# Separate tiles for the output halves, and the SSD high and low parts in one tile per group, in a hybrid LRU, attention and SSD layer

## Chip, cores and metric

The kernel runs on one core of a Trainium2 chip. The metric is the device time of one launch in microseconds: 2015.51 is the median of three runs (2010.99 to 2017.05).

## What is computed

One layer of a hybrid model for 2048 prompt tokens and 32 sample tokens (8 sequences of 4). After an RMS norm the input goes through one projection; an RG-LRU branch, a dilated attention branch and an SSD branch work on its parts, and a last projection joins them. The part that matters here, cut from the reference:

```
y, h = ssd_chunked(xs, dt, A, bm, cm, h0)          # chunks of 128 tokens, 16 heads of 64, 2 groups
ys = y + ssd_d[:, None] * xs
yg = (ys * silu(z)).reshape(B, L, 2, 512)
yg = yg * rsqrt(mean(yg * yg, axis=-1) + EPS)      # per group
y_ssd = yg.reshape(B, L, 1024) * ssd_norm_g
mix = concatenate([y_lru, y_attn, y_ssd], -1) @ w_out      # 2048 x 1024
out = x + rmsnorm(mix, post_g)
```

The outputs are `out` for prompt and samples, and new states, among them the last SSD state `ssd_h_p`.

## The kernel before

The first stages project the tokens, run the LRU and the convolutions, and the attention, and leave their results in DRAM (`d_y` for LRU and attention, `d_xbc`, `d_z`, `d_cum` for the SSD). The last stage, from about 1450 us on, does two things at once for 16 chunks of 128 tokens.

`ssd_part(c)` (from L1234) computes the SSD of chunk c in 15 steps: one to open (`ssd_open`: L669 `gp`, L672 `gm`, L678 `tpb`), then seven for each of two groups of 8 heads. In a group: `ssd_decay` loads `sg` (L649), makes `ecB` from it on ScalarE (L695) and the decay matrix (L697, L699, L700); `ssd_x` transposes and scales x (L710 to L715); TensorE makes `yd` and `yo` (L1251, L1256); VectorE forms `y` in four steps from `yo`, `ecB`, `yd`, `xb` and the gate `zt` (L1264 to L1267); `group_norm` squares it on ScalarE (L721), adds on POOL (L722, L723) and sums over partitions with a matmul by ones, `rs` (L726); then `stp` renews the state `hT` (L1273 to L1279), and the second half of `group_norm` scales `y` (L730). Last, ScalarE casts `y` to its high part (L1288) and VectorE subtracts for the low part (L1289).

`out_chunk(c)` (from L1385) multiplies the mixed features of chunk c by `w_out`, in high and low parts, three matmuls a step (`mm3`, L82 to L84). There are 32 steps, 16 blocks of 128 features for each of two halves of 512 output columns; steps 0 to 15 take LRU and attention (k below 8, both halves), steps 16 to 31 the SSD (k from 8 on, both halves). Each half is squared on ScalarE (L1445). Then comes the norm (L1448, L113, L114), and for each half an output tile `ot` is filled (L1459), the residual `xres` is added (L1460) and the tile is stored (L1461). The last chunk has its own form (L1408, L1455). `last_state` (L1463) transposes `hT` and stores it through `ho` (L1468 to L1470), for each of two groups, in step 24 of the last chunk.

The order: 15 steps of `ssd_part` go with the 32 of `out_chunk`, so the second group of chunk c is finished in the first steps of `out_chunk(c)` and the first group of chunk c + 1 in its last steps. This is the order in which the program is written. The framework plans each engine's queue when it builds the program: it takes instructions by their place in the program, but passes over those whose inputs or buffers are not ready yet in its plan. The order of each queue is fixed after that, and on the chip each engine waits at an instruction until its inputs are there.

Buffers: pool `ck` gives each tag two buffers unless told otherwise. Tag `yt` is shared by `y` of `ssd_part` and by the output tiles `ot`. `sh` and `sl` hold the high and low parts of both groups of a chunk, 4 KB per partition each. `x` holds the residuals (and raw weights at the stage's start), two buffers. `ho` has one buffer of its own.

```
y = ck.tile([128, 4, 128], F32, tag="yt", name="y")
ot = ck.tile([128, 512], F32, tag="yt", name="ot")
mh = ck.tile([128, 8, 128], F32R, tag="sh", name="sh")
h_, l_ = (mh, ml) if k < 8 else chunks[c]
ho = ck.tile([128, 4, 128], F32, tag="ho", name="ho", bufs=1)
```

Of the kernel before, what the change touches and what calls it, by code (L numbers as in the profile page):

```python
# [8 lines left out]
F32 = mybir.dt.float32  # L9
F32R = mybir.dt.float32r  # L10
AF = mybir.ActivationFunctionType
OP = mybir.AluOpType
# [20 lines left out]
def tile_hybrid_step(ctx: ExitStack, tc: tile.TileContext, A):  # L33
    nc = tc.nc
    act, dve, pool, pe, sp = nc.scalar, nc.vector, nc.gpsimd, nc.tensor, nc.sync
# [45 lines left out]
    def mm3(out, wh, wl, xh, xl, start, stop):  # L81
        pe.matmul(out, lhsT=wh, rhs=xh, start=start, stop=False)  # L82
        pe.matmul(out, lhsT=wh, rhs=xl, start=False, stop=False)  # L83
        pe.matmul(out, lhsT=wl, rhs=xh, start=False, stop=stop)  # L84
# [578 lines left out]
    def ssd_open(c, ck, ps, msk):  # L663

        t0, n = TT[c]
        bc = load_bc(ck, c)
        gp = ps["y"][0].tile([128, 2, 128], F32, tag=ps["y"][1], name="gp")
        for g in range(2):
            pe.matmul(gp[:n, g, :n], lhsT=bc[:, g], rhs=bc[:, 2 + g], start=(g == 0), stop=(g == 1),  # L669
                      skip_group_check=True)  # L670
        gm = ck.tile([128, 2, n], F32, tag="gm", name="gm", bufs=1)
        dve.tensor_tensor(out=gm[:n], in0=gp[:n, :, :n], in1=msk[:n, None, :n].to_broadcast([n, 2, n]), op=OP.mult)  # L672
        if c == 16:
            return bc, gm
        tp = ps["t"][0].tile([128, 4, 128], F32, tag=ps["t"][1], name="tpb")
        bt = ck.tile([128, 2, 128], F32, tag="bt", name="bt", bufs=1)
        for g in range(2):
            pe.transpose(tp[:, g], bc[:, g], ident)  # L678
        act.copy(out=bt, in_=tp[:, 0:2])
        return bc, gm, bt  # L680
# [51 lines left out]
    def load_z(ck, c, g):  # L732
        return load_rows4(ck, c, g, "zt", d_z)
# [6 lines left out]
    with tc.tile_pool(name="cks", bufs=1) as ck:  # L740
        ps = {"t": (psT, "tp"), "y": (psG, "g")}
# [224 lines left out]
    wo = {}  # L966
# [241 lines left out]
    chunks = {}  # L1208
# [25 lines left out]
    def ssd_part(c):  # L1234
        ck = ck0 if c == 0 else late["ck"]
        ps6 = {"t": (psA, "mm"), "y": (psA, "mm")} if c == 0 else late["ps6"]
        bc, gm, bt = ssd_open(c, ck, ps6, late["tri0" if c == 0 else "tri"])
        yield
        for g in range(2):
            hs = slice(8 * g, 8 * g + 8)  # L1240
            ecB = None if c == 0 else ck.tile([128, 4, 128], F32, tag="ecB", name="ecB", bufs=1)
            sg = ssd_decay(c, g, ck, gm, ecB)
            yield
            xb, xdt, xte = ssd_x(c, g, ck, ps6)
            pool.tensor_tensor(out=xb, in0=xb, in1=dF[:, 4 * g:4 * g + 4, None].to_broadcast([128, 4, 128]), op=OP.mult)
            yield
            hT = late["hT"]
            yd = psA.tile([128, 4, 128], F32, tag="mm", name="yd")
            for m in range(4):
                for e in range(2):  # L1250
                    pe.matmul(yd[64 * e:64 * e + 64, m], lhsT=xdt[:, 2 * m + e], rhs=sg[:, 2 * m + e],  # L1251
                              start=(m == 0), stop=(m == 3), skip_group_check=True)

            yo = None if c == 0 else psA.tile([128, 4, 128], F32, tag="mm", name="yo")
            for m in range(4 if c else 0):
                pe.matmul(yo[:, m], lhsT=hT[:, g, 128 * m:128 * m + 128], rhs=bc[:, 2 + g],  # L1256
                          start=(m == 0), stop=(m == 3), skip_group_check=True)
            yield
            zt = load_z(ck, c, g)
            y = ck.tile([128, 4, 128], F32, tag="yt", name="y")  # L1260
            if c == 0:
                dve.tensor_tensor(out=y, in0=yd, in1=xb, op=OP.add)
            else:
                dve.tensor_tensor(out=y, in0=yo, in1=ecB, op=OP.mult)  # L1264
                dve.tensor_tensor(out=y, in0=y, in1=yd, op=OP.add)
                dve.tensor_tensor(out=y, in0=y, in1=xb, op=OP.add)
            dve.tensor_tensor(out=y, in0=y, in1=zt, op=OP.mult)  # L1267
            yield
            norm = group_norm(ck, ps6, y, 128, dve if c == 0 else pool)
            next(norm)  # L1270
            yield
            stp = psA.tile([128, 512], F32, tag="mm", name="stp")
            pe.matmul(stp, lhsT=bt[:, g], rhs=xte.rearrange("p h d -> p (h d)"), start=True, stop=True)  # L1273
            if c == 0:
                act.copy(out=hT[:, g], in_=stp)
            else:
                hv = hT[:, g].rearrange("p (h d) -> p h d", d=64)
                pool.tensor_tensor(out=hv, in0=hv, in1=dec[:, c, hs, None].to_broadcast([128, 8, 64]), op=OP.mult)
                dve.tensor_tensor(out=hT[:, g], in0=hT[:, g], in1=stp, op=OP.add)  # L1279
            yield  # L1280
            for _ in norm:
                pass
            if g == 0:
                mh = ck.tile([128, 8, 128], F32R, tag="sh", name="sh")
                ml = ck.tile([128, 8, 128], F32R, tag="sl", name="sl")
                chunks[c] = mh, ml
            kk = slice(4 * g, 4 * g + 4)
            act.copy(out=mh[:, kk], in_=y)  # L1288
            dve.tensor_tensor(out=ml[:, kk], in0=y, in1=mh[:, kk].bitcast(F32), op=OP.subtract)  # L1289
            yield  # L1290

    ssd = (None for c in range(16) for _ in ssd_part(c))
# [29 lines left out]
    for i in range(16):  # L1322
# [3 lines left out]
        n = [0, 0]  # L1326
# [29 lines left out]
    ck = es.enter_context(tc.tile_pool(name="ck", bufs=2))  # L1356
# [28 lines left out]
    def out_chunk(c):  # L1385
        smp = c == 16
        t0, n = TT[c]
        if not smp:
            mh = c1.tile([128, 8, 128], F32R, tag="mh", name="mh")
            ml = c1.tile([128, 8, 128], F32R, tag="ml", name="ml")  # L1390
            for k0 in (0, 4):
                ym = load_rows4(ck, c, k0 // 4, "ym", d_y, 1)
                kk = slice(k0, k0 + 4)
                act.copy(out=mh[:, kk], in_=ym)
                dve.tensor_tensor(out=ml[:, kk], in0=ym, in1=mh[:, kk].bitcast(F32), op=OP.subtract)
        ops, ots, xres = [], [], []
# [7 lines left out]
        def scaled(hf):  # L1404

            sl = slice(512 * hf, 512 * hf + 512)
            ots.append(ck.tile([128, 512], F32, tag="yt", name="ot"))
            dve.tensor_tensor(out=ots[hf], in0=ops[hf], in1=pgB[:, sl], op=OP.mult)  # L1408
            residual(hf)

# [3 lines left out]
        for hf in range(2 if smp else 0):  # L1414

            sl = slice(512 * hf, 512 * hf + 512)
            pq = psA.tile([128, 512], F32, tag="mm", name="pq")
            for k in range(4):
                for i in range(2):
                    for j in range(4):  # L1420
                        kk = 4 * j + k
# [5 lines left out]
            ps = psO.tile([128, 512], F32, tag="o", name="ops")  # L1427
# [5 lines left out]
        for hf, k in () if smp else order:  # L1433
            if cnt[hf] == 0:
                ops.append(psO.tile([128, 512], F32, tag="o", name="ops"))
            ps = ops[hf]
            sl = slice(512 * hf, 512 * hf + 512)
            h_, l_ = (mh, ml) if k < 8 else chunks[c]
            mm3(ps[:n], h_[:, k % 8, :n], l_[:, k % 8, :n], wo[k][0][:, sl], wo[k][1][:, sl],
                cnt[hf] == 0, cnt[hf] == 15)  # L1440
            cnt[hf] += 1
            yield
            if cnt[hf] == 16:
                jk = ck.tile([128, 512], F32, tag="zt", name="jk")
                act.activation(out=jk[:n], in_=ps[:n], func=AF.Square, accum_out=oss[:n, hf:hf + 1])  # L1445
                if c == 15:
                    scaled(hf)
        dve.tensor_tensor(out=oss[:n, 0:1], in0=oss[:n, 0:1], in1=oss[:n, 1:2], op=OP.add)  # L1448
        r = rstd_of(sm, oss[:, 0:1], DM, n, "ro")
        for hf in range(2):  # L1450
            sl = slice(512 * hf, 512 * hf + 512)
            dst = A["y_prompt"][0, t0:t0 + n, sl] if not smp else A["y_sample"].rearrange("b l d -> (b l) d")[:, sl]
            if c == 15:
                ot = ots[hf]
                dve.scalar_tensor_tensor(out=ot, in0=ot, scalar=r, in1=xres[hf], op0=OP.mult, op1=OP.add)  # L1455
            else:
                residual(hf)
                ot = ck.tile([128, 512], F32, tag="yt", name="ot")
                dve.scalar_tensor_tensor(out=ot[:n], in0=ops[hf][:n], scalar=r[:n], in1=pgB[:n, sl], op0=OP.mult, op1=OP.mult)  # L1459
                dve.tensor_tensor(out=ot[:n], in0=ot[:n], in1=xres[hf][:n], op=OP.add)  # L1460
            sp.dma_start(out=dst, in_=ot[:n])  # L1461

    def last_state():  # L1463
        for g in range(2):
            tp = psT.tile([128, 4, 128], F32, tag="tp", name="tpf")
            for j in range(4):
                pe.transpose(tp[:, j], hT[:, g, 128 * j:128 * j + 128], ident)
            ho = ck.tile([128, 4, 128], F32, tag="ho", name="ho", bufs=1)  # L1468
            act.copy(out=ho, in_=tp)
            sp.dma_start(out=A["ssd_h_p"][0, 0, 8 * g:8 * g + 8].rearrange("(m e) p n -> (e p) m n", e=2), in_=ho)  # L1470

# [9 lines left out]
    for c in range(16):  # L1481
        k = 0
# [115 lines left out]
```

## Time and profile before

| what | value |
|---|---|
| median of three runs | 2015.51 us (2010.99 to 2017.05) |
| the profiled execution | 2012.49 us, span 2010.6 us |
| busy TensorE, VectorE, ScalarE, POOL | 1925.6, 1066.6, 742.7, 279.2 us |
| mean DMA rate over the span | 110 GB/s |
| mean granted TensorE clock | 0.990 |

The span is the time from the first to the last instruction of the program; all times in the rows count from its start. The profile names an instruction by its line in the kernel, its engine, and the tiles it writes and reads. PE is TensorE, DVE VectorE, ACT ScalarE, SP the engine that issues the DMAs here.

### The profile page before, as it was taken

How to read it: one execution, taken by the hardware profiler on the slowest of the kernel's cores; microseconds unless marked ns; L12 is line 12 of the kernel's file. 1: busy time of each engine (PE TensorE's matmuls, PEld its weight loads, DVE VectorE, ACT ScalarE, POOL GpSimd, SP SyncE). 2: the span in 40 equal slices, each digit the busy share in tenths (PEclk: the TensorE clock that was granted, in tenths of full speed). 3: DMA queues.
4: the chain of work that ended last, by engine and by line, in shares of the span. 5: the costliest groups of instructions: out<-in, count | busy, mean ns of one | idle time of the engine just before them, and what ended most of it. 6: DMA issues, size and time to landing. Idle time of an engine off the chain costs nothing.

```text
span 2010.6 us, 35818 instructions
## 1 busy us (share of the span) xinstructions
PE 1925.6 (96%) x14218; PEld 1569.0 (78%) x14218; DVE 1066.6 (53%) x2314; ACT 742.7 (37%) x1464; POOL 279.2 (14%) x346
## 2 busy tenths in 40 slices
PE   7999999999999999999999889999988999989998
PEld 7998888888888888887877667777756777567776
DVE  7315433434323666664223236666767676566664
ACT  6311525252422222223234235556543333333332
POOL 0100101111001111110001000000122232222221
PEclk9999999999999999999999999999999999999999
DMA  8322111111233222225377664334554434234341
GB/s 244 116 75 62 54 54 59 48 61 55 87 93 97 66 73 71 78 69 158 106 208 206 185 176 129 101 102 133 166 157 132 129 112 129 83 108 130 110 126 63
DMA packets 277106, 221.75 MB, mean 110 GB/s; under 512 B 33458, under 2 KB 233122, under 8 KB 276940
## 3 DMA queue, kind: packets, MB, share of 16 engines
q1 hardware_dynamic: 276940, 219.47, 36.2%
q8 instruction: 112, 1.84, 0.4%
q14 instruction: 54, 0.44, 0.1%
HBM read 150.55 MB, written 68.86 MB: 109 GB/s over the span
## 4 chain that ended last, share of the span: by engine, by line
PE 70%; DVE 9%; DMA 8%; ACT 6%; issue 4%; POOL 2%; SPq 1%; DVEq 0%; POOLq 0%; ACTq 0%
PE mm L82 15%; PE mm L83 15%; PE mm L84 15%; PE pt L1142 3%; DMA out_dram<-ot 2%; PE o L1178 2%; ACT sr L1114 2%; PE s L1087 2%; PE ops L83 2%; PE ops L84 2%; PE ops L82 2%; PE s L1066 1%; PE mmt L82 1%; PE mmt L83 1%; PE mmt L84 1%
## 5 line engine op out<-in xcount | busy, mean ns | idle before, releaser
L82 PE MATMUL mm<-xh,wh 128*128 128x512 f32 (+2 forms) x1600 | 563.9, 352 | 0.0
L83 PE MATMUL mm<-xl,wh 128*128 128x512 f32 (+2 forms) x1600 | 560.9, 351 | 0.0
L84 PE MATMUL mm<-xh,wl 128*128 128x512 f32 (+2 forms) x1600 | 560.2, 350 | 0.0
L82 PEld LDWEIGHTS mm<-xh,wh 128*128 128x128 f32 x1600 | 301.6, 188 | 40.7 <-issue 2.9
L83 PEld LDWEIGHTS mm<-xl,wh 128*128 128x128 f32 x1600 | 301.4, 188 | 39.8 <-issue 2.5
L84 PEld LDWEIGHTS mm<-xh,wl 128*128 128x128 f32 x1600 | 300.7, 188 | 38.7 <-issue 1.2
L146 POOL TENSOR_TENSOR wr<-wr,gC 128x1024 f32<-128x1024 f32 x40 | 78.7, 1967 | 398.1 <-DMA wr<-in_w_in_dram 351.4
L439 DVE SCALAR_TENSOR_TENSOR o<-u,ssdc,o 128x512 f32<-128x512 f32 (+1 forms) x216 | 122.8, 590 | 5.1
L148 DVE SCALAR_TENSOR_TENSOR wl<-wr,wh 128x1024 fp32r<-128x1024 f32 x40 | 48.9, 1223 | 120.4 <-ACT wh L147 120.4
L1114 ACT ACTIVATE sr<-sr,nm 128x384 f32<-128x384 f32 (+3 forms) x128 | 97.9, 771 | 23.3 <-DVE nm L1110 14.1
L619 ACT ACTIVATE o<-o 128x512 f32<-128x512 f32 (+2 forms) x60 | 33.1, 552 | 149.9 <-DVE o L439 78.0
L437 DVE TENSOR_SCALAR o<-u,ssdc 128x512 f32<-128x512 f32 (+1 forms) x72 | 47.2, 669 | 65.0 <-ACT u L419 56.8
L1025 ACT COPY ptsb<-pt 128x512 f32<-128x512 f32 x96 | 52.4, 583 | 75.4 <-PE pt L1142 75.3
L82 PE MATMUL mmt<-wh,xh 128*128 128x256 f32 (+3 forms) x272 | 79.2, 293 | 1.0 <-ACT xh L250 0.6
L695 ACT ACTIVATE ecB<-sg 64x512 f32<-64x512 f32 x60 | 37.8, 630 | 113.3 <-DVE y L1264 92.7
L84 PE MATMUL mmt<-wh,xl 128*128 128x256 f32 (+3 forms) x272 | 78.4, 289 | 0.0
L83 PE MATMUL mmt<-wl,xh 128*128 128x256 f32 (+3 forms) x272 | 77.9, 288 | 0.0
L1142 PE MATMUL pt<-ident,sr 128*128 128x128 f32 x576 | 75.2, 281 | 2.3 <-ACT sr L1114 1.8
L1142 PEld LDWEIGHTS pt<-ident,sr 128*128 128x128 f32 x576 | 63.7, 143 | 14.6 <-issue 8.8
L697 DVE TENSOR_SCALAR sg<-sg,cum 128x128 f32<-128x128 f32 (+1 forms) x256 | 70.0, 337 | 5.4 <-ACT ecB L695 5.2
L1087 PE MATMUL s<-k,q 64*32 64x256 f32 (+1 forms) x1536 | 68.9, 348 | 3.8 <-DVE mx L1075 3.2
L1091 DVE CUSTOM_DVE_ANT_0 sr<-s,bias 128x128 f32<-128x128 f32 (+3 forms) x128 | 58.8, 486 | 25.2 <-PE s L1087 24.1
(534 smaller groups left out, 3565.4 us busy)
## 6 DMA issues: line engine op xcount, KB each, us to landing
wr<-in_w_in_dram SPq DMA_DIRECT2D x40, 512.0 KB
sg<-d_cum SPq DMA_DIRECT2D x30, 512.0 KB
d_xbc<-o SPq DMA_DIRECT2D x36, 256.0 KB
x<-in_x_prompt_dram SPq DMA_DIRECT2D x32, 256.0 KB
vt<-in_cache_attn_v_dram SPq DMA_DIRECT2D x32, 256.0 KB
kc<-in_cache_attn_k_dram SPq DMA_DIRECT2D x32, 256.0 KB
xres<-in_x_prompt_dram SPq DMA_DIRECT2D x32, 256.0 KB
out_dram<-ot SPq DMA_DIRECT2D x32, 256.0 KB
```

Source lines behind the costliest of these rows:

```text
L82: pe.matmul(out, lhsT=wh, rhs=xh, start=start, stop=False)
L83: pe.matmul(out, lhsT=wh, rhs=xl, start=False, stop=False)
L84: pe.matmul(out, lhsT=wl, rhs=xh, start=False, stop=stop)
L146: pool.tensor_tensor(out=wr, in0=wr, in1=gC[:, :, None].to_broadcast([128, 8, 128]), op=OP.mult)
L148: dve.scalar_tensor_tensor(out=wl, in0=wr, scalar=scale, in1=wh.bitcast(F32), op0=OP.mult, op1=OP.subtract)
L439: dve.scalar_tensor_tensor(out=o, in0=v(t), scalar=w[:, t:t + 1], in1=o, op0=OP.mult, op1=OP.add)
L697: dve.tensor_scalar(out=sg[:n, h], in0=sg[:n, h], scalar1=cum[:n, c, 8 * g + h:8 * g + h + 1], scalar2=0.0, op0=OP.subtract, op1=OP.min)
L1025: act.copy(out=out, in_=in_)
L1087: pe.matmul(ps[e][32 * n:32 * n + 32, 256 * h:256 * h + m], lhsT=qr[hd[e], r, 32 * n:32 * n + 32], rhs=krs[h][hd[e], r, 0:m // 32], start= ...
L1091: dve.tensor_tensor_reduce(out=sr[e][r][:, :nk], in0=ps[e][:, :nk], in1=bs[:, e, 512 - nk:512], scale=1.0, scalar=NEG, op0=OP.add, op1=OP. ...
L1114: act.activation(out=sr[e][r], in_=sr[e][r], func=AF.Exp, bias=nm[:, e, r:r + 1], accum_out=ll[:, e, r:r + 1])
L1142: pe.transpose(tp[:, r], sr[e][r][:, 128 * g:128 * g + 128], ident)
```

## The change

It touches the last stage alone. The output tiles `ot` get a tag of their own, with two buffers, in both places where they are made. The high and low parts get one tile per group instead of one per chunk: two buffers for the first group, one for the second; the matmuls pick the tile of the group. `ho` takes the tag `x`, with its two buffers, in place of its own. Per partition the parts shrink from 16 to 12 KB, the output tiles add 4 KB, and `ho` gives up 2 KB.

```diff
-            if g == 0:
-                mh = ck.tile([128, 8, 128], F32R, tag="sh", name="sh")
-                ml = ck.tile([128, 8, 128], F32R, tag="sl", name="sl")
-                chunks[c] = mh, ml
-            kk = slice(4 * g, 4 * g + 4)
-            act.copy(out=mh[:, kk], in_=y)
-            dve.tensor_tensor(out=ml[:, kk], in0=y, in1=mh[:, kk].bitcast(F32), op=OP.subtract)
+
+            mh, ml = [ck.tile([128, 4, 128], F32R, tag=f"s{i}{g}", name=f"s{i}", bufs=2 - g) for i in "hl"]
+            chunks[c, g] = mh, ml
+            act.copy(out=mh, in_=y)
+            dve.tensor_tensor(out=ml, in0=y, in1=mh.bitcast(F32), op=OP.subtract)
...
-            ots.append(ck.tile([128, 512], F32, tag="yt", name="ot"))
+            ots.append(ck.tile([128, 512], F32, tag="ot", name="ot"))
...
-            h_, l_ = (mh, ml) if k < 8 else chunks[c]
-            mm3(ps[:n], h_[:, k % 8, :n], l_[:, k % 8, :n], wo[k][0][:, sl], wo[k][1][:, sl],
+            h_, l_ = (mh, ml) if k < 8 else chunks[c, k // 4 - 2]
+            j = k if k < 8 else k % 4
+            mm3(ps[:n], h_[:, j, :n], l_[:, j, :n], wo[k][0][:, sl], wo[k][1][:, sl],
...
-                ot = ck.tile([128, 512], F32, tag="yt", name="ot")
+                ot = ck.tile([128, 512], F32, tag="ot", name="ot")
...
-            ho = ck.tile([128, 4, 128], F32, tag="ho", name="ho", bufs=1)
+            ho = ck.tile([128, 4, 128], F32, tag="x", name="ho", bufs=2)
```

## Rows read from the trace of the kernel before

**Rows 1.** The page, part 1: busy time, share of span, instructions per engine.

```profile
PE 1925.6 (96%) x14218; PEld 1569.0 (78%) x14218; DVE 1066.6 (53%) x2314; ACT 742.7 (37%) x1464; POOL 279.2 (14%) x346
```

**Rows 2.** Windows: stretch, length, busy time by engine, granted clock, DMA share, GB/s.

```profile
1505.00:1981.00 476.00, 443.79 (x2428) 337.26 (x2427) 324.14 (x600) 165.25 (x337) 134.72 (x143) 0.99 0.38 116
1632.00:1664.00 32.00, 30.60 (x167) 23.77 (x167) 22.82 (x43) 11.44 (x23) 9.64 (x11) 1.00 0.39 120
1781.00:1817.00 36.00, 32.00 (x167) 24.83 (x166) 22.79 (x43) 11.53 (x23) 9.49 (x11) 0.95 0.36 111
```

**Rows 3.** Waits from 1500 to 2000 us: total, times, longest.

```profile
DVE y L1264 <- DMA out_dram<-ot: 37.0, 12, 5.2
PE rs L726 <- POOL sq L723: 30.6, 28, 3.6
DVE y L1264 <- PE yo L1256: 13.5, 13, 1.1
DVE y L1264 <- PE ops L84: 7.6, 3, 2.6
```

**Rows 4.** Timeline of one chunk: start, length, instruction, idle before.

```profile
1599.63 1.54 DVE L1460 TENSOR_TENSOR ot<-ot,xres 128x512 f32<-128x512 f32 x2
...
1600.60 0.95 SPq L1461 DMA_DIRECT2D out_dram<-ot  x2
...
1603.85 0.69 DVE L1264 TENSOR_TENSOR y<-yo,ecB 128x512 f32<-128x512 f32 x1 [2.67 <-DMA out_dram<-ot]
...
1608.90 0.51 POOL L723 TENSOR_TENSOR sq<-sq 128x128 f32<-128x128 f32 x1
...
1609.47 0.49 PE L726 MATMUL rs<-sq,ones 128*128 128x128 f32 x2 [0.99 <-POOL sq L723]
```

**Rows 5.** Timeline of TensorE: some `rs` with idle time before them.

```profile
1517.35 0.49 PE L726 MATMUL rs<-sq,ones 128*128 128x128 f32 x2 [2.36 <-POOL sq L723]
...
1530.74 0.49 PE L726 MATMUL rs<-sq,ones 128*128 128x128 f32 x2 [1.01 <-POOL sq L723]
...
1793.14 0.49 PE L726 MATMUL rs<-sq,ones 128*128 128x128 f32 x2 [3.56 <-POOL sq L723]
...
1972.12 0.49 PE L726 MATMUL rs<-sq,ones 128*128 128x128 f32 x2 [0.37 <-POOL sq L723]
...
1988.80 0.38 PE L726 MATMUL rs<-sq,ones 128*128 128x128 f32 x1 [0.32 <-POOL sq L723]
```

**Rows 6.** The chain that ended last, from 1500 us: start, length, what.

```profile
1584.24 3.84 DMA sg<-d_cum
...
1600.60 3.12 DMA out_dram<-ot
...
1781.71 5.70 DMA out_dram<-ot
...
1981.09 2.05 DMA out_dram<-ot
```

**Rows 7.** Windows of 6 us after two idle stretches, columns as in rows 2.

```profile
1793.00:1799.00 6.00, 5.86 (x24) 4.84 (x25) 3.27 (x5) 2.67 (x5) 1.06 (x2) 0.72 0.00 0
...
1576.00:1582.00 6.00, 4.60 (x25) 3.96 (x26) 4.49 (x8) 2.84 (x6) 2.56 (x4) 1.00 0.11 33
```

**Rows 8.** Timeline of the last chunk: residual loads, second `ho`, last adds.

```profile
1982.09 0.95 SPq L1402 DMA_DIRECT2D xres<-in_x_prompt_dram  x2
...
2001.66 0.59 ACT L1469 COPY ho<-tpf 128x512 f32<-128x512 f32 x1 [2.44 <-DMA out_dram<-ho]
...
2005.98 1.42 DVE L1455 SCALAR_TENSOR_TENSOR ot<-ot,rstd,xres 128x512 f32<-128x512 f32 x2 [0.60 <-ACT rstd L114]
```

**Rows 9.** Timeline of a chunk with a store of 4.57 us: SP, VectorE, ScalarE.

```profile
1662.14 1.57 SPq L649 DMA_DIRECT2D sg<-d_cum  x1
...
1664.08 1.28 DVE L1460 TENSOR_TENSOR ot<-ot,xres 128x512 f32<-128x512 f32 x2
...
1670.21 1.28 ACT L695 ACTIVATE ecB<-sg 64x512 f32<-64x512 f32 x2 [7.49 <-DVE y L1264]
```

## The prediction

> **What bounds the kernel now.** I read the page first: TensorE is busy 96% of the span, VectorE 53% [rows 1]. The last quarter is the output stage, where the change lies, so I took it by windows: from 1505 to 1981 us TensorE stands for 32.2 of 476 us. A plain chunk lasts 32 us with 30.6 busy; some last 36, at a mean granted clock of 0.95 [rows 2]. Then the waits of that stretch [rows 3]: VectorE's first multiply of `y` (L1264) waits 37.0 us in 12 times for the landing of an output store, and TensorE waits 30.6 us in 28 times for the squares that feed `rs` (L726). Three more waits of L1264, 7.6 us, stand under a matmul, but they follow a store in the same way, so I count 15.
>
> How the two belong together shows in one chunk [rows 4]. VectorE ends the last output add at 1601.17; `y` shares its two buffers with the output tiles, so it waits for a store issued at 1600.60 and starts at 1603.85, 2.67 us idle. From there, four VectorE steps, the square on ScalarE and two POOL adds lead to `rs` at 1609.47, where TensorE has stood 0.99 us. TensorE is the bound, and this chain is the one that reaches it late.
>
> The idle time follows the store one for one [rows 4 to 6]: a store of 5.70 us gives 3.56, of 3.12 gives 0.99, of 2.05 gives 0.32. In the plain chunks it is the store less 2.13 us: `rs` stands at a fixed place in TensorE's queue, behind the matmul of wo4h, chosen when the program was built, and a store of 2.13 us would just keep up with it.
>
> **The change part by part. The output tiles get buffers of their own (L1407, L1458).** `y` then waits only for the `y` two groups before and starts when VectorE is free, at 1601.17 instead of 1603.85. What goes: the 15 idle stretches ahead of the second group's `rs`, from 2.36 us (the first) to 0.32 (the last) [rows 5]. They sum to 22.9 us: the other 13 of the 28 sum to 7.7, from 1.01 to 0.37, and 30.6 - 7.7 = 22.9. That is 1.53 each.
>
> Not all of it goes. The planner that orders the queues will see `y` ready earlier too and will put `rs` further forward, so what is left is by how much its chain without a store lags behind the plan. No row shows that. The lower bound is 0. The upper one is about 1.0, the largest idle of an `rs` that no store gates. The nearest rows are those first-group `rs` of the plain chunks, whose wait includes a load of `ym` instead: 0.37 to 0.57 in nine of the 13. I take 0.45. The gain is 15 x (1.53 - 0.45) = **16.2 us**, between 8 and 23.
>
> **The clock.** Behind the idle stretches of 2.36, 2.44, 3.56 and 2.60 us the granted clock over 6 us is 0.72, which is a stretch at the lower level, 1.2 GHz; behind one of 2.79 us it stays at 1.00 [rows 7]. One costs 0.28 x 6 = 1.7 us, four 6.7. All four stand behind long stores. Taken as gone: **6.7 us**, between 3.4 (two stay) and 6.7.
>
> The size of the store can be weighed against a page. The rows have stores of 2.05 to 5.70 us between issue and the release of `y`. The Trainium skill, DMA: Bandwidth & Descriptors, section Anatomy of one DMA — SWDGE (gpsimd) path, gives a fixed 2.0 us plus the bytes over 436 GB/s, so 2.6 us is its estimate for 256 KB, if it holds for stores that SP issues. By that each idle stretch would be 2.6 - 2.13 = 0.5 us, 7 us in all with no long store and no clock to win back, and the forecast would be no better than 2006. The rows decide against it.
>
> **High and low parts in two tiles per group (L1284 to L1289, L1438).** The casts, subtractions and matmuls stay the same in number and shape. The second group has one buffer, so its cast (L1288) must follow the last matmul of the chunk before that reads it. That matmul is the last of its chunk and lies before the output adds of 1599.63; `rs`, which the cast needs through `y`, runs on the same TensorE queue at 1609.47 [rows 4]. The order holds already, by almost 10 us. Cost 0; at most a semaphore more per group on VectorE, whose idle time covers it. The first group keeps two buffers.
>
> **The last state (L1468) on the buffers of the residual.** Now the second `ho` is copied at 2001.66, after the first has been stored, and both residual loads of the last chunk were issued at 1982.09 [rows 8]. If these hold both buffers, `ho` must wait until the last adds release them, from 2005.98 to 2007.4: copy 0.59, the second pair of transposes and copy, and stores issued near 2007.5 and 2009 instead of a last store near 2007.4. That is 1.8 us on the end. If `ho` comes first, the second residual load waits for its stores, and the last add is at most 0.5 us late. Bounds 0 and 2; I take **+1**.
>
> Addresses of the tiles that follow move by up to 4 KB, so some first loads of the stage can wait for other attention tiles. No row prices it; the nearest is the first idle stretch of the stage, 2.36 us [rows 5], which bounds it either way. I take 0, since such a load waits once and not per chunk.
>
> Sum: 16.2 + 6.7 - 1 = 21.9 us. The profiled execution took 2012.49 us (span 2010.6), 3.0 below the median of 2015.51. From it: 2012.5 - 21.9 = 1990.6. I say 1991 and don't add the 3 us, since scatter from long stores should shrink with the change.
>
> **What is late next.** `y` free of the store meets the load of `sg`. In the chunk of rows 9 it is issued at 1662.14 and at 3.84 us [rows 6] lands at 1666.0, or as much as 1.57 later by the issue's own length. ScalarE makes `ecB` from it once L1264 has read the old one: now at 1670.21, and without the store 0.69 after the adds that end at 1665.36, so at 1666.1 [rows 9]. That slack of 4 us is spent almost whole, and ScalarE runs this step ahead of the square.
>
> **The rivals.** *The order's lag lies in the chain.* If 1.0 us of idle stays per chunk, the gain is 15 x 0.53 + 6.7 - 1 = 13.7 and the time 1999. For it: ungated `rs` of up to 1.01 exist [rows 5]; against: most are near half of that.
>
> *The load of sg takes the store's place.* If it lands later than some 5 us after issue, the square waits behind it; 0.8 us more per chunk costs 12 of the 22: 2003. For it: the spent slack; against: 3.84 us as seen.
>
> *More goes than the stores' part.* With `y` early, `ym` and the first group's chain could also move up: idle 0 at the second group's `rs` and 5 of the 7.7 us: 22.9 + 6.7 + 5 = 34.6, and 1978.
>
> *It gets slower.* Mechanism: the planner puts `rs` too far forward, because its plan no longer holds a store that gave the real chain time. Place: each second-group `rs`. It decides from a mean idle of over 1.53 us. At 2.5 us, the clock falls in each of 15 chunks too: 15 x 0.97 + 11 x 1.7 + 1 = 34, so 2047. Against it: the chain's lag as far as rows show is a few tenths.
>
> *It does nothing measurable.* `y` would have to wait for something else until the same moment, such as its own earlier buffer or TensorE's `yo`. For it: L1264 also waits 13.5 us in 13 other times for `yo` [rows 3]; against: 37.0 us of its waits end with a store, whose length the idle time follows. 2012.
>
> **How the numbers follow.** Forecast 0.46; lag in the chain 0.16; sg 0.12; more than the stores 0.13; nothing 0.07; slower 0.06. A measurement of this kernel can tell about 0.3%, 6 us, from no change. Faster: 0.46 + 0.16 + 0.12 + 0.13 = 0.87; same 0.07; slower 0.06. The range goes from 1978 (the largest gain) to 2006 (sg at its price and 3 us for the median above the profiled time), and holds the first four cases.
>
> **What would show it.** Right: L1264 waits for no output store; the second group's `rs` idles under 0.6 us in most chunks, at an earlier matmul than wo4h; chunks of 31 us without the 36 us ones; granted clock 1.00 between 1520 and 1980; the end's `ho` near the last store. Wrong: `rs` idle near 1 us or more at its new place, ScalarE waiting for `sg`, or a clock still falling.

## The result, and the profile after

The changed kernel takes 1992.26 us (median of three runs, 1987.44 to 1992.82) against 2015.51: a ratio of the means of 0.9882, with a 95% interval of 0.9848 to 0.9917. The forecast was 1991. Run again beside the last experiment it took 1993.57 (six runs, 1988.54 to 2006.70), a ratio of 0.9924 (0.9897 to 0.9951). The kernel before, run beside the experiments, had medians of 2011.79 us (first four) and 2011.37 us (the last, and this repeat); the ratios below are to these runs. The profiled execution took 1992.26 us with a span of 1990.4, so 20.2 less than the profiled one of before.

After the change some lines have moved: the cast and subtraction of the parts are L1286 and L1287, the output add L1459, the store L1460, the residual load L1400, the last adds L1454. Lines up to L1279 are as before.

The page of the changed kernel, part 1, shows the same work in a shorter span:

```profile
PE 1927.8 (97%) x14218; PEld 1571.4 (79%) x14218; DVE 1061.0 (53%) x2314; ACT 743.5 (37%) x1464; POOL 270.7 (14%) x346
```

Windows of the changed kernel (stretch, length, busy time by engine, granted clock, DMA share, GB/s): the output stage, a plain chunk, a long one, and 6 us inside the long one.

```profile
1505.00:1960.00 455.00, 440.95 (x2433) 335.43 (x2434) 315.84 (x590) 165.18 (x338) 128.90 (x143) 1.00 0.39 121
1603.00:1634.00 31.00, 30.68 (x168) 23.94 (x167) 22.49 (x42) 11.63 (x24) 9.23 (x10) 1.00 0.41 128
1766.00:1801.00 35.00, 32.25 (x174) 25.26 (x172) 22.61 (x42) 11.71 (x25) 8.95 (x11) 0.95 0.38 113
1777.00:1783.00 6.00, 5.70 (x22) 4.89 (x23) 3.04 (x5) 2.52 (x5) 0.24 (x1) 0.72 0.00 1
```

TensorE stands for 14.1 us of the stage where it stood for 32.2 [rows 2]. A plain chunk lasts 31 us instead of 32. One chunk of 35 us is left, and it has the one stretch of the stage at the lower clock.

The waits from 1500 to 1980 us (total, times, longest):

```profile
ACT ecB L695 <- DMA sg<-d_cum: 56.9, 22, 6.6
DVE y L1264 <- PE yo L1256: 20.6, 14, 1.6
PE rs L726 <- POOL sq L723: 12.7, 19, 2.7
DVE sg L697 <- ACT ecB L695: 5.6, 7, 2.3
```

And, beside [rows 3], two lines of before, from 1500 to 2000 us:

```profile
ACT ecB L695 <- DVE y L1264: 92.7, 14, 8.7
ACT ecB L695 <- DMA sg<-d_cum: 13.6, 12, 4.1
```

The line of L1264 and the output store [rows 3] is gone. TensorE's idle time at `rs` fell from 30.6 to 12.7 us. ScalarE's idle time at `ecB`, mostly for L1264 before (92.7 us), is now mostly for the load of `sg`: 56.9 us where it was 13.6.

A plain chunk in the timeline (start, length, instruction, idle before it), to be set beside [rows 4]:

```profile
1592.92 0.45 SPq L649 DMA_DIRECT2D sg<-d_cum  x1
...
1594.89 1.28 DVE L1459 TENSOR_TENSOR ot<-ot,xres 128x512 f32<-128x512 f32 x2
...
1595.60 0.95 SPq L1460 DMA_DIRECT2D out_dram<-ot  x2
...
1596.09 0.68 DVE L1264 TENSOR_TENSOR y<-yo,ecB 128x512 f32<-128x512 f32 x1
...
1597.31 1.28 ACT L695 ACTIVATE ecB<-sg 64x512 f32<-64x512 f32 x2 [3.78 <-DMA sg<-d_cum]
...
1600.71 0.51 POOL L723 TENSOR_TENSOR sq<-sq 128x128 f32<-128x128 f32 x1
...
1601.27 0.49 PE L726 MATMUL rs<-sq,ones 128*128 128x128 f32 x2 [0.34 <-POOL sq L723]
```

`y` starts 0.49 us after the store is issued, as soon as VectorE has ended the adds; before, 3.25 us passed. `rs` now stands behind the first step of the second half of the columns (wo0h) in TensorE's queue instead of in the fifth (wo4h): the planner did move it forward. What remains is 0.34 us where it was 0.99.

The long chunk shows what holds `rs` up now:

```profile
1766.66 0.84 SPq L649 DMA_DIRECT2D sg<-d_cum  x1
...
1769.76 0.68 DVE L1264 TENSOR_TENSOR y<-yo,ecB 128x512 f32<-128x512 f32 x1
...
1771.27 0.69 DVE L1266 TENSOR_TENSOR y<-y,xb 128x512 f32<-128x512 f32 x1
...
1773.57 1.28 ACT L695 ACTIVATE ecB<-sg 64x512 f32<-64x512 f32 x2 [6.64 <-DMA sg<-d_cum]
1774.24 0.28 DVE L697 TENSOR_SCALAR sg<-sg,cum 128x128 f32<-128x128 f32 x1 [2.28 <-ACT ecB L695]
1774.44 0.68 DVE L1267 TENSOR_TENSOR y<-y,zt 128x512 f32<-128x512 f32 x1
...
1776.73 0.51 POOL L723 TENSOR_TENSOR sq<-sq 128x128 f32<-128x128 f32 x1
...
1777.30 0.49 PE L726 MATMUL rs<-sq,ones 128*128 128x128 f32 x2 [2.68 <-POOL sq L723]
```

The load takes 6.9 us from issue to use. VectorE's queue has the first step on `sg` (L697) between the third and the fourth step of `y`, so `y` waits 2.28 us for a load that belongs to the next group, and TensorE 2.68 us.

### The profile page after: what moved, and what is told of

It reads as the page before. It is cut to its first block, busy times and chain, and to the rows that moved or that the text cites. A ratio compares the mean times of both kernels' runs of the same rounds, so it can differ in the third digit from the quotient of the medians.

```text
span 1990.4 us, 35805 instructions
## 1 busy us (share of the span) xinstructions
PE 1927.8 (97%) x14218; PEld 1571.4 (79%) x14218; DVE 1061.0 (53%) x2314; ACT 743.5 (37%) x1464; POOL 270.7 (14%) x346
## 4 chain that ended last, share of the span: by engine, by line
PE 79%; DVE 6%; DMA 5%; ACT 5%; issue 2%; POOL 1%; SPq 0%; POOLq 0%; ACTq 0%; DVEq 0%
PE mm L82 15%; PE mm L83 15%; PE mm L84 15%; PE ops L83 3%; PE ops L84 3%; PE ops L82 3%; PE pt L1142 3%; PE o L1178 2%; DMA sg<-d_cum 2%; PE s L1087 2%; ACT sr L1114 2%; PE s L1066 1%; PE mmt L82 1%; PE mmt L83 1%; PE mmt L84 1%
## 5 line engine op out<-in xcount | busy, mean ns | idle before, releaser
L439 DVE SCALAR_TENSOR_TENSOR o<-u,ssdc,o 128x512 f32<-128x512 f32 (+1 forms) x216 | 127.3, 611 | 5.1
L437 DVE TENSOR_SCALAR o<-u,ssdc 128x512 f32<-128x512 f32 (+1 forms) x72 | 42.3, 601 | 65.4 <-ACT u L419 57.0
L697 DVE TENSOR_SCALAR sg<-sg,cum 128x128 f32<-128x128 f32 (+1 forms) x256 | 68.4, 328 | 10.1 <-ACT ecB L695 10.1
L147 ACT ACTIVATE wh<-wr 128x1024 fp32r<-128x1024 f32 x40 | 42.4, 1061 | 75.1 <-PE mm L83 67.8
```

What stands on the lines that cost most here:

```text
L439: dve.scalar_tensor_tensor(out=o, in0=v(t), scalar=w[:, t:t + 1], in1=o, op0=OP.mult, op1=OP.add)
L697: dve.tensor_scalar(out=sg[:n, h], in0=sg[:n, h], scalar1=cum[:n, c, 8 * g + h:8 * g + h + 1], scalar2=0.0, op0=OP.subtract, op1=OP.min)
```

## The experiments

**y's buffers alone.** The kernel before, with three buffers on the shared tag and `ho` on the residual's buffers to make room.

```diff
-            y = ck.tile([128, 4, 128], F32, tag="yt", name="y")
+            y = ck.tile([128, 4, 128], F32, tag="yt", name="y", bufs=3)
...
-            ho = ck.tile([128, 4, 128], F32, tag="ho", name="ho", bufs=1)
+            ho = ck.tile([128, 4, 128], F32, tag="x", name="ho", bufs=2)
...
-                ot = ck.tile([128, 512], F32, tag="yt", name="ot")
+                ot = ck.tile([128, 512], F32, tag="yt", name="ot", bufs=3)
```

(The other `ot` likewise.)

> The kernel before with one more buffer on the tag that y and the output tiles share (three instead of two) and ho on the residual's buffers; high and low parts as before, in one tile per chunk. Theory (the gain comes from y no longer waiting for an output store, in whatever way its buffer comes free): no wait of L1264 for an output store, about 1992 us, within 6. Rival (the split of the high and low parts carries the gain): about 2012 to 2016.

It took 1994.58 us, a ratio of 0.9921 (0.9893 to 0.9949). Its waits from 1500 to 1980 us have no line of L1264 and a store, and read much like those of the changed kernel:

```profile
ACT ecB L695 <- DMA sg<-d_cum: 54.3, 20, 5.9
PE rs L726 <- POOL sq L723: 15.6, 22, 2.0
```

So a buffer that is free in time is enough, and the old parts with two buffers per group give nothing beyond it: the second group's single buffer costs nothing that can be seen.

**The parts alone.** The changed kernel with the output tiles back on the tag of `y`:

```diff
-            ots.append(ck.tile([128, 512], F32, tag="ot", name="ot"))
+            ots.append(ck.tile([128, 512], F32, tag="yt", name="ot"))
...
-                ot = ck.tile([128, 512], F32, tag="ot", name="ot")
+                ot = ck.tile([128, 512], F32, tag="yt", name="ot")
```

> The changed kernel with the output tiles put back on y's two buffers: the split of the parts and ho's move alone. Theory: L1264 waits some 37 to 45 us for output stores again, 2011 to 2017 us. Rival (the split carries the gain): about 1992. If the single buffer of the second group cost anything, it would be above 2017.

It took 2015.69 us; the ratio to the kernel before is 1.0025 (1.0008 to 1.0042). Its waits from 1500 to 2000 us are much like those of [rows 3]:

```profile
DVE y L1264 <- DMA out_dram<-ot: 41.6, 13, 4.6
PE rs L726 <- POOL sq L723: 31.9, 27, 2.9
```

Alone, the split of the parts and the move of `ho` give nothing; by the ratio they cost 2 to 8 us. The two profiled executions differ by 3.6 us. Of these 2.9 stand ahead of the first matmul with `w_out`, which the change doesn't touch, and 1.0 in the last chunk, where the second residual load waits for the stores of `ho` and the last add 0.58 us for it; what lies between adds up to -0.4. What is left of the split is the 4 KB per partition that it frees; whether the tiles would fit without them, no run shows.

**The store left out.** The kernel before, without the output stores of prompt chunks 0 to 14:

```diff
-            sp.dma_start(out=dst, in_=ot[:n])
+            if smp or c == 15:
+                sp.dma_start(out=dst, in_=ot[:n])
```

> The kernel before without the output stores of prompt chunks 0 to 14 (their rows of y_prompt are left unwritten), y and the output tiles still on two shared buffers. Theory (the landing of the store is the whole of y's wait, and the sharing as such costs nothing): about 1990 us, a little under the changed kernel if the stores also slow the load of sg. Rival (y waits because it shares with tiles that VectorE still fills): over 2005.

It took 1991.30 us, a ratio of 0.9907 (0.9882 to 0.9933). Waits from 1500 to 1980 us:

```profile
ACT ecB L695 <- DMA sg<-d_cum: 49.1, 19, 5.3
PE rs L726 <- POOL sq L723: 14.1, 22, 1.4
DVE y L1264 <- DMA out_dram<-ot: 1.8, 1, 1.8
```

With the shared buffers kept and the stores gone, the time is that of the changed kernel. The landing of the store is thus the whole price of the sharing. The wait for `sg` is nearly as long as with the stores (49.1 against 56.9 us). Where ScalarE waits for it, the load takes 3.7 to 5.7 us from issue to use, 4.2 in the middle one; in the changed kernel it is 3.8 to 6.9, and 4.2 in the middle one. So the stores are not the main reason why it lands late; whether they make the longest loads longer is not shown. (The one store wait left is that of the sample rows.)

**ho on its own buffer.** The changed kernel with this line of before:

```diff
-            ho = ck.tile([128, 4, 128], F32, tag="x", name="ho", bufs=2)
+            ho = ck.tile([128, 4, 128], F32, tag="ho", name="ho", bufs=1)
```

> The changed kernel with ho on one buffer of its own again. Theory: in the last chunk both residual loads are issued early, near the last store of the chunk before, the last output add no longer waits 0.46 us for its residual, and the end comes 0.5 us sooner: 1991 to 1992 us, not to be told from the changed kernel by time, but by the rows of the end. Rival (ho's place costs 2 us or more): 1990 or less.

It took 1988.65 us, 0.9899 (0.9872 to 0.9926), whose interval overlaps both of those of the changed kernel; by time it isn't told apart. The rows of the end tell. First those of the changed kernel:

```profile
1961.53 0.44 SPq L1400 DMA_DIRECT2D xres<-in_x_prompt_dram  x1
...
1978.60 3.38 SPq L1469 DMA_DIRECT2D out_dram<-ho  x2
...
1983.91 0.35 SPq L1400 DMA_DIRECT2D xres<-in_x_prompt_dram  x1
...
1986.54 0.75 DVE L1454 SCALAR_TENSOR_TENSOR ot<-ot,rstd,xres 128x512 f32<-128x512 f32 x1 [0.46 <-DMA xres<-in_x_prompt_dram]
```

Then those of the experiment:

```profile
1955.79 0.95 SPq L1400 DMA_DIRECT2D xres<-in_x_prompt_dram  x2
...
1979.59 1.42 DVE L1454 SCALAR_TENSOR_TENSOR ot<-ot,rstd,xres 128x512 f32<-128x512 f32 x2 [0.60 <-ACT rstd L114]
```

On the shared buffers `ho` came first and the second residual load waited for its store, until 1983.91; the last add then stands 0.46 us. With a buffer of its own both loads go at 1955.79 and the two adds run without a gap. From the first matmul of the last chunk to the end 24.9 us pass, against 25.4 in the changed kernel: `ho`'s place costs 0.5 us, as the theory had it, and the 2 us of the rival are not there. The rest of its lower time lies elsewhere: from 1500 us on its longest idle stretch at `rs` is 1.2 us where the changed kernel had 2.68, and the clock doesn't fall before 1979 us. Up to the last chunk the two programs are written alike, so that may be scatter between executions; one profile of each doesn't show it.

**Two buffers for sg.** The changed kernel with a second buffer for `sg`; the room comes from `y` and the output tiles on one tag with three buffers, which the first experiment showed to be as good.

```diff
-        sg = ck.tile([128, 8, n], F32, tag="sg", name="sg", bufs=1)
+        sg = ck.tile([128, 8, n], F32, tag="sg", name="sg", bufs=2)
...
-            y = ck.tile([128, 4, 128], F32, tag="yt", name="y")
+            y = ck.tile([128, 4, 128], F32, tag="yt", name="y", bufs=3)
...
-                ot = ck.tile([128, 512], F32, tag="ot", name="ot")
+                ot = ck.tile([128, 512], F32, tag="yt", name="ot", bufs=3)
```

> The changed kernel with two buffers for sg; to make room, the output tiles go back on y's tag, with three buffers there. Theory (what still holds rs up is the load of sg, whose one buffer comes free only when the matmuls of the group before have read it): ScalarE's waits for sg, 56.9 us in 22 times, nearly vanish, the second group's rs idles about 0.3 us in every chunk, so that of its 11 us some 6 go, with the stretch at the lower clock, and the time is 1983 to 1987 us. Rival (the lag lies in the plan of the chain itself, whatever the loads do): within 2 us of the changed kernel.

Beside it, on the same chip, the changed kernel once more:

> The changed kernel once more, beside the others: 1987 to 1994 us by either theory. It shows how far the long idle stretches and the stretches at the lower clock differ from one execution to the next.

With two buffers it took 1984.93 us, 0.9884 (0.9863 to 0.9904) of the kernel before; the changed kernel took 1993.57, 0.9924 (0.9897 to 0.9951). So the second buffer gives 8.6 us by the medians, and this is the lowest median here; but the two intervals touch, and the changed kernel's first ratio, 0.9882, was as low. The profiles say how much of it is idle time. The 15 stretches at the second group's `rs` sum to 7.5 us; in the changed kernel's two profiles they sum to 11.0 and 12.1, with one fall of the clock in each, where here there is none. At 1.7 us for a fall, that is 5 to 6 us. The expectation of 6 us of idle time gone was too high. Its waits from 1500 to 1980 us have no line of `ecB` and the load of `sg`:

```profile
ACT ecB L695 <- DVE y L1264: 50.4, 15, 3.5
PE rs L726 <- POOL sq L723: 10.2, 21, 1.1
```

And a chunk of it:

```profile
1576.72 0.46 SPq L649 DMA_DIRECT2D sg<-d_cum  x1
...
1590.41 0.45 SPq L649 DMA_DIRECT2D sg<-d_cum  x1
...
1593.51 0.68 DVE L1264 TENSOR_TENSOR y<-yo,ecB 128x512 f32<-128x512 f32 x1
...
1594.22 1.29 ACT L695 ACTIVATE ecB<-sg 64x512 f32<-64x512 f32 x2 [3.54 <-DVE y L1264]
...
1598.76 0.49 PE L726 MATMUL rs<-sq,ones 128*128 128x128 f32 x2 [0.40 <-POOL sq L723]
```

`ecB` now starts when `y` lets go of the old one: its load was issued at 1576.72, and the one of 1590.41 is already that of the next group. The chunks from the fourth on last 30.9 to 31.5 us, apart from the one with the samples and the one behind it (32.0), and the clock doesn't fall between 1500 and 1979. In the changed kernel's two profiles three and four chunks of this stretch took 32 to 35 us. What is left is 0.40 us at the second group's `rs` in a plain chunk, ahead of which neither `ecB` nor L697 waits for a load: the lag of the chain behind its plan. No run changed that; whether another way to square and add would shorten it was not tried.

## Why the prediction was right

**The mechanism held.** Every step of the chain shows as it was put: no output store ahead of L1264, `rs` at an earlier place, plain chunks of 31 us. The store left out and the three shared buffers both show that the landing of the store, not the tag or the parts, was the price. One pair that I set beside the others doesn't follow the rule of the store less 2.13 us: by it a store of 2.05 us leaves no idle time, and 0.32 stood there. That `rs` is the last chunk's, behind wo3h instead of wo4h; the rule holds for one place in the queue.

**The terms.** Of the idle time at the second group's `rs` I took 22.9 us down to 15 x 0.45 = 6.8, a gain of 16.2. The 15 stretches of the changed kernel sum to 11.0, so the gain was 11.9. Eight are 0.22 to 0.38, below the 0.45, and four 0.46 to 0.78; three long ones, 2.68, 1.66 and 1.45, are most of what was missed. They are the rival that the load of `sg` takes the store's place, and in part it came true: before each of the three, L697 waited for `ecB` and the load (2.28, 1.25 and 1.05 us). All that stands above 0.33 us a stretch is 11.0 - 15 x 0.33 = 6 us. With two buffers for `sg` 3.5 of them and the fall of the clock are gone, and no stretch but the first two (1.08 and 1.14 us, and much the same with three shared buffers) is over 0.67.

The path of that rival was put wrongly in one point. I had ScalarE run `ecB` ahead of the square and so hold it up. The longer hold is on VectorE, whose queue has a step on `sg` ahead of the last step of `y`.

**The clock.** I took four stretches at the lower clock as gone, 6.7 us. [rows 7] has one of them; these are the other three in the kernel before, in the same columns:

```profile
1673.00:1679.00 6.00, 3.90 (x14) 3.38 (x15) 3.85 (x10) 2.61 (x5) 1.27 (x2) 0.72 0.17 45
1892.00:1898.00 6.00, 5.66 (x23) 4.68 (x24) 3.08 (x5) 2.61 (x5) 1.07 (x2) 0.72 0.00 0
1516.00:1522.00 6.00, 4.65 (x22) 3.89 (x24) 4.08 (x5) 2.50 (x5) 2.97 (x3) 0.72 0.19 51
```

One remained in the profiled execution, behind the 2.68 us: 5.0 us gained.

**The first group's rs** I left at its 7.7 us, and gave 5 of them to a rival of its own. This half of the rival came true: these waits went from 13 to four, with 0.94 us the longest and 1.7 in all, a gain of 6.0. Why the first group's chain comes sooner was not looked for; its `rs` stands behind the same matmul (wo9h) as before. With this, three terms sum to 11.9 + 6.0 + 5.0 = 22.9, and the forecast's two were 16.2 + 6.7 = 22.9: the misses offset each other by luck, and the forecast is nearer than its terms were.

**The end.** I allowed 1 us, between `ho` first, at most 0.5, and `ho` last, 1.8. It was `ho` first, with 0.46. That leaves 22.4 for a span that fell by 20.2. The rest lies ahead of the steady chunks. The first matmul with `w_out` starts 0.8 us later, and from it to the first of the second chunk 62.0 us passed in this profile and 60.0 before, but 60.3 in the second profile of the changed kernel and 59.0 with two buffers for `sg`. I don't put that down to the change.

**The rival on the slower side**, `rs` placed too far forward, didn't occur: its mean idle is 11.0 / 15 = 0.73 us, against 1.53 before. **The estimate from the Trainium skill**, DMA: Bandwidth & Descriptors, section Anatomy of one DMA — SWDGE (gpsimd) path, of 2.6 us for every store, gave 2006 at best. The traces don't agree with it: the stores of before took 2.05 to 5.70 us [rows 6], and the changed kernel took 1992.26.

## What to carry to other kernels

When the bound engine idles at one place chunk after chunk, set each idle stretch beside the length of each transfer in the chain that leads to it: if one follows the other with a constant difference, as long as the waiting instruction keeps its place in the queue, the transfer is the likely cause, and the difference tells how much of it the order already covers. A tile that is released by a store should not share too few buffers with one that starts a chain; here one more buffer on the shared tag did the same as a tag of its own. And before a wait is removed, work out the slack of the next transfer in that chain: here 4 us of slack on `sg` were spent at a stroke, and a second buffer there took off another 8.6 us by the medians, of which 5 to 6 show as idle time and clock.

## What the runs showed of the hardware

Transfers of one size differ much from one time to the next: the 256 KB stores took 2.05 to 5.70 us in the profile of before, and the 512 KB load of `sg` 4.4 us in the plain chunk and 6.9 in the long one after the change. So a place that waits for a transfer has a few long chunks and many plain ones, and the long ones cost more than their wait, since the granted clock fell behind most of them: after 2.36, 2.44, 2.60 and 3.56 us idle before the change and after 2.68 us with it, though not after one of 2.79 us [rows 7]. In the run with the parts alone it fell after 2.13, 2.38, 2.67 and 2.85 us and not after 2.70 and 2.94, and with three shared buffers after 1.97. No length of the idle time parts the two in these runs. A fall cost about 1.7 us: 0.28 of the 6 us of a window.
